# Three score blocks of a head pair, side by side instead of two projection steps apart

## The chip, the cores and the metric

The kernel runs on one core of one Trainium2 chip. The metric is the device time of one execution in microseconds (us), the median of three runs.

The core has a matrix engine (TensorE, PE in the profile; PEld is its weight load), a vector engine (VectorE, DVE), a scalar engine (ScalarE, ACT), a general engine (GpSimd, POOL) and a queue engine that issues transfers (SyncE, SP). Each engine works through its own list of instructions in order, and waits where an instruction needs what another engine has not yet finished.

## What is computed

The program is one layer of a hybrid decoder trunk over 1024 positions of width 1024. The part that matters here is the second of its two token mixers, a gated linear attention in chunks:

```python
def step(state, chunk):
    qc, kc, lfc, vc = chunk
    cum = jnp.cumsum(lfc, axis=2)
    o_inter = jnp.einsum('bhtk,bhkv->bhtv', qc * jnp.exp(cum), state)
    rel = cum[:, :, :, None, :] - cum[:, :, None, :, :]
    decay = jnp.where(causal[:, :, None], jnp.exp(jnp.minimum(rel, 0.0)), 0.0)
    scores = jnp.einsum('bhtsk,bhsk->bhts', qc[:, :, :, None, :] * decay, kc)
    o_intra = jnp.einsum('bhts,bhsv->bhtv', scores, vc)
    ...
    return state, o_inter + o_intra
```

Queries q, keys k, forget gates f and values v come from projections of the normalised input (`proj = h @ w_in`). Beside this mixer there are a gated recurrence (RG-LRU), an output projection, and then an MLP with squared ReLU (1024 to 4096 to 1024). All inputs are float32.

## The kernel before

The 1024 positions are worked in two halves of 512 (c = 0, 1), and the 8 heads in 4 pairs (p = 0 to 3). So the mixer goes through 8 head pairs, one after the other; the names of their tiles carry both numbers (`sc_10` is c = 1, p = 0), and the text counts them 0 to 7 in the order of time (4c + p).

Every float32 product of the projections is made of three matmuls of reduced operands (lines 144, 145, 146: high by high, high by low, low by high). While pair i goes through its attention (`hgrn`), TensorE also makes the projections of pair i + 1. These are cut into steps by a generator (`stage`): a step is six such matmuls of 128x512 (of 128x256 in the value projection). `hgrn` calls `go(n)` to run n steps of the next pair's projections, and then places its own small matmuls. The tables `GO`, `GO_FIRST` and `GO_SECOND_HALF` say how many steps go before each of them. While the mixer runs, all matmuls are pinned (`pin`, line 141): TensorE takes them in exactly the order of the program text. The other engines' orders are made by a scheduler from priorities.

The score matrix of 128 by 128 of one chunk is built in levels. For distances inside a pair of positions and for two coarser levels there are three score blocks, each made by `blocks` (line 570): 32 matmuls with 32 columns of weights and 48 columns moving. On the chip each of these is two passes, so a block is 64 matmul records.

- The first block (here pt1) reads `q` and `kk`, the second (pt2) `qa` and `kb`, the third (pt8) `qb` and `kc`. Each goes to a PSUM bank of its own (pt1 and pt2 of the two banks `sc`, pt8 of the two banks `hg`).
- VectorE then takes the blocks out of PSUM into `dd` with masks (`own_block`, lines 560 and 581; `level_blocks`, line 589), and at the same time it rewrites `kc`, `qb`, `kk` and `qf` for the next, coarser level. GpSimd copies `dd` into `scT` (line 675).
- After `at[1]` further steps come the blocks of the two coarsest levels (line 690, 32 columns wide; line 701, 64 columns wide), then the transposes of `kk` (`pk`, line 727), the products with v (`pkv`, line 737) and the outputs (`po`, lines 762 and 765).

In the first half the table has 26, so pt1 comes after 22 steps, pt2 after 24 and pt8 after 26. From pair 1 on, the first 16 of these steps are the value projection, the next 8 `xa`, and then `q` follows; `f` and the recurrence's gates (`pr`, `pi`) come behind. In the last pair, gates `g` and `mb` stand in the place of `xa` and what follows it.

Of the kernel before, what the change touches and what calls it, by code (L numbers as in the profile page):

```python
# [35 lines left out]
GO = (26, 5, 3, 1, 1)  # L36
GO_FIRST = (16, 5, 2, 1, 2)
GO_SECOND_HALF = (26, 7, 3, 1, 1)


PV_LB, PV_CB, PV_BR, PV_BI, PV_LAM, PV_CW, PV_HG = 0, 8, 16, 24, 32, 40, 72
# [4 lines left out]
def trunk(ctx: ExitStack, tc: tile.TileContext, x, wts, mlp, pv, gains, mask_f, mask_u, out):  # L46
# [15 lines left out]
    def bank(tag, name):  # L62
        return ps.tile([P, 512], F32, tag=tag, name=name, bufs={"pj": 4, "sc": 2, "hg": 2}[tag])
# [3 lines left out]
    for i in range(NC * NPAIR):  # L67
        at = (0, 1, 2, 3, 4, 6, 5)
# [487 lines left out]
    def hgrn(c, p, got, go):  # L556
# [6 lines left out]
        def blocks(k_, rhs, name, tag="sc"):  # L563

            pt = bank(tag, f"sc{name}_{nm}")[:, : 8 * 48].rearrange("p (n t) -> p n t", n=8)
            for n in range(8):
                for b in range(4):
                    k = 4 * n + b
                    pin(
                        PE.matmul(  # L570
                            pt[32 * b : 32 * b + 32, n, :], k_[:, 32 * k : 32 * k + 32], rhs(k), start=True, stop=True
                        )
                    )
            return pt
# [48 lines left out]
        def level_q(q4, t4, g, cw):  # L623
            mul(q4[:, :, 5, :], q4[:, :, 3, :], t4[:, :, 2:3].to_broadcast([P, g, cw]))
            mul(q4[:, :, 4:7:2, :], q4[:, :, 2:6:3, :], t4[:, :, 1:2].unsqueeze(3).to_broadcast([P, g, 2, cw]))
# [20 lines left out]
        q4 = qb.rearrange("p a (b c) -> p a b c", c=c1)  # L646
        level_q(q4, t4, g1, c1)
        at = GO_FIRST if first else GO_SECOND_HALF if c else GO
        between = 2
        go(at[0] - 2 * between)  # L650
        pt1 = blocks(kk, lambda k: q1[:, 16 * k : 16 * k + 16, :], "1")
        go(between)
        pt2 = blocks(kb, lambda k: qa[:, k * g0 // 32 : (k + 1) * g0 // 32, 1:7, :], str(c0))
        go(between)
        pt8 = blocks(kc, lambda k: q4[:, k * g1 // 32 : (k + 1) * g1 // 32, 1:7, :], str(c1), "hg")
        before, after = sums(t4, g1)
        mul(k4(kc, c1)[:, :, 0:3, :], k4(kc, c1)[:, :, 0:3, :], after.unsqueeze(3).to_broadcast([P, g1, 3, c1]))
# [23 lines left out]
                op1=ALU.add,  # L681
            )

        go(at[1])
        pt = bank("hg", f"sc32_{nm}")[:, :256].rearrange("p (n t) -> p n t", n=8)
        for n in range(8):
            for b in (0, 2):
# [70 lines left out]
        for s, u in both:  # L758
            for n in range(4):
# [3 lines left out]
                if not only:  # L763
                    at = s * T + n * P
# [177 lines left out]
    for i in range(NC * NPAIR):  # L942
        rest = stage(i + 1) if i + 1 < NC * NPAIR else last_stage()
        hgrn(*where(i), gots[i], lambda n: run(rest, n))
        run(rest)
# [704 lines left out]
```

## Time and profile before

| what | us |
|---|---|
| median of 3 runs | 1545.02 |
| lowest and highest of the 3 | 1544.61, 1545.6 |
| profiled execution, first to last instruction | 1544.2 |
| TensorE busy in it | 1527.6 (99%) |
| VectorE busy | 1150.0 (74%) |
| ScalarE busy | 810.2 (52%) |
| GpSimd busy | 149.8 (10%) |

The profiled execution has no time of its own beside its span; the span counts from its first to its last instruction and lies 0.8 us below the median of the runs. The mixer takes about the first 560 us, then follow the rest of the gates, the output projection and the MLP. In the timeline a row is one instruction, or a run of like ones (x64), with its start and how long it took. Matmuls are pipelined: a new one starts before the last has ended, so the distance between two starts tells more than the time of one.

### The profile page before, as it was taken

The page shows a single profiled execution, that of the slowest core. Times are in us where ns is not written, and L with a number is a line of the kernel's source. Part 1 is how long each engine was busy: PE and PEld are TensorE (multiplying, and loading weights), DVE is VectorE, ACT ScalarE, POOL GpSimd, SP SyncE. Part 2 cuts the span into 40 slices and gives each one's busy share as a digit, 9 for nine tenths or more (in the row PEclk, how much of TensorE's full clock was granted, in tenths as well). Part 3 has the DMA queues.
Part 4 walks back from the last instruction along what each step waited for, and adds up shares of the span by engine and source line. Part 5 has one row for each costly group of instructions (what it writes and reads, how often), then busy time and mean ns, then how long its engine had stood idle before and what let it go on. Part 6 is the DMA issues. An engine that isn't in the chain of part 4 may idle for free. (4 is left out here: it accounts for less than half of the span.)

```text
span 1544.2 us, 23190 instructions
## 1 busy us (share of the span) xinstructions
PE 1527.6 (99%) x9081; PEld 1275.3 (83%) x9081; DVE 1150.0 (74%) x1656; ACT 810.2 (52%) x1341; POOL 149.8 (10%) x188
## 2 busy tenths in 40 slices
PE   8999999999999999999999999999999999999998
PEld 7878888888888887888888888888888788888886
DVE  5798595485675928786866568888788898888877
ACT  5647757568567435453533347766666721111115
POOL 1021210233515600000000000000000000000000
PEclk9999999999999999999999999999999999999999
DMA  7555455465664274432328323666666675666642
GB/s 285 188 173 192 151 190 182 151 218 172 236 212 158 96 286 164 164 135 84 137 94 314 151 109 143 267 247 246 244 249 248 228 312 224 249 252 250 252 186 109
DMA packets 81679, 306.82 MB, mean 199 GB/s; under 512 B 8481, under 2 KB 20897, under 8 KB 68642
## 3 DMA queue, kind: packets, MB, share of 16 engines
q1 hardware_dynamic: 77536, 292.75, 51.8%
q10 hardware_dynamic: 4034, 12.59, 2.1%
q8 instruction: 71, 1.16, 0.3%
q14 instruction: 38, 0.31, 0.1%
HBM read 201.50 MB, written 103.81 MB: 198 GB/s over the span
## 5 line engine op out<-in xcount | busy, mean ns | idle before, releaser
L1559 DVE TENSOR_TENSOR acc<-acc,dX 128x512 f32<-128x512 f32 x128 | 85.0, 683 | 28.6 <-PE dX L146 26.9
L87 ACT CAST wA<-q 128x512 fp32r<-128x512 f32 x46 | 28.6, 622 | 147.5 <-PE dX L146 101.7
L88 DVE TENSOR_TENSOR wL<-raw,wH 128x1024 fp32r<-128x1024 f32 x48 | 58.8, 1225 | 46.0 <-ACT wH L87 45.7
L87 ACT CAST wH<-raw 128x1024 fp32r<-128x1024 f32 x48 | 50.4, 1050 | 39.4 <-DMA raw<-wts_in 16.1
L1559 DVE TENSOR_TENSOR acc<-acc,dY 128x512 f32<-128x512 f32 x64 | 43.4, 685 | 13.1 <-PE dY L146 12.9
L144 PE MATMUL po<-wH,y 128*128 128x512 f32 x128 | 49.8, 393 | 0.0
L145 PE MATMUL po<-wL,y 128*128 128x512 f32 x128 | 49.8, 389 | 0.0
L146 PE MATMUL po<-wH,y 128*128 128x512 f32 x128 | 49.7, 390 | 0.0
L1420 ACT ACTIVATE b<-b 128x512 f32<-128x512 f32 x48 | 30.2, 630 | 32.2 <-DVE b L1419 32.0
L88 DVE TENSOR_TENSOR wA<-q,wA 128x512 fp32r<-128x512 f32 x46 | 31.5, 686 | 16.6 <-ACT wA L87 16.4
L108 ACT CAST wH<-raw 128x1024 fp32r<-128x1024 f32 x36 | 37.7, 1048 | 9.8 <-issue 3.7
L465 DVE SCALAR_TENSOR_TENSOR xc<-xp,pvt,xc 128x512 f32<-128x512 f32 x48 | 40.1, 846 | 1.1 <-ACT xc L449 1.1
L171 POOL TENSOR_TENSOR rstd_h<-rstd_h,mhalf 128x1 f32<-128x1 f32 x8 | 4.6, 584 | 371.9 <-DVE rstd_h L166 371.9
L981 DVE TENSOR_TENSOR s<-q,q 128x512 f32<-128x512 f32 x46 | 31.6, 686 | 4.4 <-DMA q<-mlp_in 4.0
L378 POOL TENSOR_TENSOR stt<-r,stt 128x256 fp32r<-128x256 f32 x16 | 19.9, 1261 | 127.6 <-ACT stt L377 115.4
L989 DVE TENSOR_TENSOR s<-q 128x512 f32<-128x512 f32 x46 | 31.6, 686 | 0.4
L1421 ACT ACTIVATE b<-b 128x512 f32<-128x512 f32 x48 | 30.2, 631 | 1.2
L769 ACT ACTIVATE on<-po 128x128 f32<-128x128 f32 x64 | 16.9, 278 | 26.1 <-PE po L765 26.0
L1071 DVE TENSOR_TENSOR gb<-gY,ge 128x512 f32<-128x512 f32 x14 | 9.7, 690 | 25.1 <-PE gY L146 25.1
L146 PEld LDWEIGHTS po<-wH,y 128*128 128x128 f32 x128 | 24.0, 188 | 5.1
L145 PEld LDWEIGHTS po<-wL,y 128*128 128x128 f32 x128 | 24.1, 188 | 4.8
L144 PEld LDWEIGHTS po<-wH,y 128*128 128x128 f32 x128 | 24.0, 188 | 4.7
(2546 smaller groups left out, 5448.9 us busy)
## 6 DMA issues: line engine op xcount, KB each, us to landing
q<-mlp_in SPq DMA_DIRECT2D x92, 512.0 KB, 3.8
raw<-wts_in SPq DMA_DIRECT2D x80, 512.0 KB, 4.9
rest<-wL SPq DMA_DIRECT2D x36, 512.0 KB, 2.9
wL<-rest SPq DMA_DIRECT2D x36, 512.0 KB, 4.2
hd<-ri SPq DMA_DIRECT2D x16, 256.0 KB, 3.7
od<-onT ACTq DMA_DIRECT2D x8, 512.0 KB, 7.3
cdT<-stT SPq DMA_DIRECT2D x16, 256.0 KB, 3.4
o<-od SPq DMA_DIRECT2D x4, 1024.0 KB, 6.8
```

What stands on the lines that cost most here:

```text
L87: keep(A.copy(h, src))
L88: ins = V.tensor_tensor(out=lo, in0=src, in1=h.bitcast(F32), op=ALU.subtract)
L108: A.copy(h, raw)
L144: pin(PE.matmul(o, ah, bh, start=first, stop=False, **how))
L145: pin(PE.matmul(o, ah, bl, start=False, stop=False, **how))
L146: pin(PE.matmul(o, al, bh, start=False, stop=last, **how))
L465: ins = V.scalar_tensor_tensor(xc[:, s, :], xp[:, j : j + T], pvt[:, PV_CW + 8 * j + u : PV_CW + 8 * j + u + 1], xc[:, s, :], op0=ALU.mult ...
L981: ins = V.tensor_tensor(out=sa[:, 0, :], in0=a21, in1=a22, op=ALU.add)
L989: V.tensor_tensor(out=sb[:, 0, :], in0=a21, in1=a11, op=ALU.add)
L1420: A.activation(b[:, at, :], b[:, at, :], AF.Relu, scale=-1.0 if at == 2 else 1.0)
L1421: A.activation(b[:, at, :], b[:, at, :], AF.Square)
L1559: V.tensor_tensor(out=dst, in0=dst, in1=banks[bk, pr], op=op)
```

## The change

The same matmuls, vector operations and transfers remain. A new table moves the three score blocks among the projection steps:

```diff
+SCORES_AT = {0: (0, 2, 2), 2: (3, 0, 0), 7: (3, 0, 0)}
...
         at = GO_FIRST if first else GO_SECOND_HALF if c else GO
-        between = 2
-        go(at[0] - 2 * between)
+        before_1, before_2, before_8 = SCORES_AT.get(4 * c + p, (0, 0, 0))
+        go(at[0] - 4 + before_1)
         pt1 = blocks(kk, lambda k: q1[:, 16 * k : 16 * k + 16, :], "1")
-        go(between)
+        go(before_2)
         pt2 = blocks(kb, lambda k: qa[:, k * g0 // 32 : (k + 1) * g0 // 32, 1:7, :], str(c0))
-        go(between)
+        go(before_8)
         pt8 = blocks(kc, lambda k: q4[:, k * g1 // 32 : (k + 1) * g1 // 32, 1:7, :], str(c1), "hg")
...
-        go(at[1])
+        go(at[1] + 4 - before_1 - before_2 - before_8)
```

| pair | steps before pt1, pt2, pt8: before | after |
|---|---|---|
| 0 | 12, 14, 16 | 12, 14, 16 |
| 1, 3, 4, 5, 6 | 22, 24, 26 | 22, 22, 22 |
| 2, 7 | 22, 24, 26 | 25, 25, 25 |

The blocks behind them (line 690 and on) keep their step in every pair, since the last line gives back what the others took.

On TensorE, in pair 4 (`sc_10`), the three blocks stood so among the projections of `xa` and `q`, with 12 matmuls of 128x512 between one block and the next:

```order
L146 MATMUL pj_xa_1_3558<-hT11H,wL_3429 128x512
L570 MATMUL sc_10_3607<-q_3187,kk_3384 32x48 x32
L144 MATMUL pj_xa_0_3557<-hT11H,wH_3428 128x512
...
L146 MATMUL pj_xa_1_3558<-hT11H,wL_3429 128x512
L570 MATMUL sc_10_3659<-qa_3395,kb_3397 32x48 x32
L144 MATMUL pj_q_0_3715<-hT10H,wH_3561 128x512
...
L146 MATMUL pj_q_1_3716<-hT10H,wL_3562 128x512
L570 MATMUL sc_10_3735<-qb_3401,kc_3409 32x48 x32
L144 MATMUL pj_q_0_3715<-hT10H,wH_3561 128x512
```

Now they stand so (line numbers are one higher, because of the new line of the table):

```order
L147 MATMUL pj_xa_1_3558<-hT11H,wL_3429 128x512
L571 MATMUL sc_10_3607<-q_3187,kk_3384 32x48 x32
L571 MATMUL sc_10_3640<-qa_3395,kb_3397 32x48 x32
L571 MATMUL sc_10_3673<-qb_3401,kc_3409 32x48 x32
L145 MATMUL pj_xa_0_3557<-hT11H,wH_3428 128x512
```

All 24 projection matmuls that stood between the blocks have gone behind the third.

On VectorE, in the same pair, the operations that take the blocks out of PSUM (`dd`) stood mixed with the convolution of the next pair (`xc`, line 465), ahead of the rewriting of `kc` and `qb`:

```order
L581 COPY_PREDICATED dd_3392<-mu,sc_10_3607 128x128
L463 COPY xp_3656<-xcar 128x3
L589 COPY_PREDICATED dd_3392<-mu,sc_10_3659 128x32x6
L465 SCALAR_TENSOR_TENSOR xc_3652<-xp_3653,pvt,xc_3652 128x512
L589 COPY_PREDICATED dd_3392<-mu,sc_10_3659 128x32x4
L465 SCALAR_TENSOR_TENSOR xc_3652<-xp_3653,pvt,xc_3652 128x512
L589 COPY_PREDICATED dd_3392<-mu,sc_10_3659 128x32x2
L465 SCALAR_TENSOR_TENSOR xc_3652<-xp_3653,pvt,xc_3652 128x512
L465 SCALAR_TENSOR_TENSOR xc_3652<-xp_3656,pvt,xc_3652 128x512
L463 COPY xp_4357<-xcar 128x3
L465 SCALAR_TENSOR_TENSOR xc_3652<-xp_3656,pvt,xc_3652 128x512
L560 TENSOR_TENSOR kc_3409<-kc_3409,seg_3394 128x32x24
```

Now they stand so:

```order
L582 COPY_PREDICATED dd_3392<-mu,sc_10_3607 128x128
L590 COPY_PREDICATED dd_3392<-mu,sc_10_3640 128x32x6
L590 COPY_PREDICATED dd_3392<-mu,sc_10_3640 128x32x4
L590 COPY_PREDICATED dd_3392<-mu,sc_10_3640 128x32x2
L561 TENSOR_TENSOR kc_3409<-kc_3409,seg_3394 128x32x24
L561 TENSOR_TENSOR qb_3401<-qb_3401,seg_3394 128x32x8
L561 TENSOR_TENSOR qb_3401<-qb_3401,seg_3394 128x32x16
L561 TENSOR_TENSOR kk_3384<-kc_3409,seg_3394 128x16x32
L561 TENSOR_TENSOR qf_3717<-qb_3401,seg_3394 128x16x32
L590 COPY_PREDICATED dd_3392<-mu,sc_10_3673 128x8x24
L464 COPY xp_3748<-xcar 128x3
L590 COPY_PREDICATED dd_3392<-mu,sc_10_3673 128x8x16
```

The convolution has moved behind the work on the three blocks. Ahead of the first of these rows, that is up to the last operation that pt8 needs, VectorE's order in this pair is as it was.

## The prediction

> **What bounds the kernel now.** I read the page's first part, then the busy times by stretch, then TensorE's waits. In the stretches the columns are the stretch, its length, and the busy time and count of each engine (PE, PEld, DVE, ACT, POOL), then the granted clock and the transfers.
>
> ```profile
> PE 1527.6 (99%) x9081; PEld 1275.3 (83%) x9081; DVE 1150.0 (74%) x1656; ACT 810.2 (52%) x1341; POOL 149.8 (10%) x188
> ...
> 75.00:560.00 485.00, 482.60 (x4433) 414.85 (x4432) 339.41 (x586) 304.76 (x618) 139.41 (x161) 1.00 0.53 182
> 560.00:1300.00 740.00, 738.25 (x3271) 606.70 (x3270) 568.68 (x693) 399.82 (x565) 4.64 (x8) 1.00 0.53 196
> ...
> PE po L762 <- DVE sn L748: 1.0, 1, 1.0
> PE dZ L145 <- DVE wA1230L L88: 0.5, 1, 0.5
> PE sc L701 <- DVE qf L560: 0.5, 1, 0.5
> ```
>
> TensorE is busy for 482.6 of the 485 us in which the head pairs run, and for 738.25 of the 740 us behind them, at full clock. It waits for almost nothing: behind its start the largest wait is 1.0 us. So what TensorE is given in this stretch sets the end, and time that it is spared there should reach the end nearly whole, since the 740 us that follow are full too and nothing in their order has moved. A wait that it is given costs the same way. But a busy share does not say how fast it goes; that is read from starts. Pair 4, from its first score block to its third:
>
> ```profile
> 327.64 0.39 PE L145 MATMUL pj_xa<-hT11L,wH 128*128 128x512 f32 x1
> 327.86 0.39 PE L146 MATMUL pj_xa<-hT11H,wL 128*128 128x512 f32 x1
> 328.18 0.89 PE L570 MATMUL sc<-q,kk 128*32 128x48 f32 x64
> 329.00 0.50 PE L144 MATMUL pj_xa<-hT11H,wH 128*128 128x512 f32 x1
> 329.34 0.40 PE L145 MATMUL pj_xa<-hT11L,wH 128*128 128x512 f32 x1
> ...
> 330.03 0.39 PE L145 MATMUL pj_xa<-hT11L,wH 128*128 128x512 f32 x1
> ...
> 331.62 0.39 PE L146 MATMUL pj_xa<-hT11H,wL 128*128 128x512 f32 x1
> 331.94 0.89 PE L570 MATMUL sc<-qa,kb 128*32 128x48 f32 x64
> ...
> 335.70 0.89 PE L570 MATMUL sc<-qb,kc 128*32 128x48 f32 x64
> ...
> L570 PE MATMUL sc<-q,kk x512: 206/206/230, 84.6 to 513.5; 128*32 128x48 f32 x171
> ```
>
> Undisturbed projections start every 0.227 us (330.03 to 331.62 are seven starts: 1.59 / 7). From block to block it takes 3.76 us, and again 3.76, with 12 projections between: 12 x 0.227 = 2.72. A block that stands alone therefore costs 3.76 - 2.72 = **1.04 us**. Its 64 records themselves, first start to last start, take 0.89 less the last one's own 0.206, that is **0.68 us**. The other **0.36 us** is the way in and out: the first record comes 0.32 us behind the last projection instead of 0.227, the first projection comes late, and the second comes 0.34 us behind the first.
>
> **The change, part by part.** It removes no instruction and no transfer. In pairs 1 to 7 the three blocks now have one way in and one way out between them instead of three. Two are spared in each of seven pairs, 14 in all; pair 0 keeps its 12, 14, 16. By the rows above that is worth 14 x 0.36 = 5.0 us, if a border between two score blocks costs nothing beyond the records' pace.
>
> In pair 2 the first block already shares a border, with the eight transposes of the input rows:
>
> ```profile
> 197.09 0.39 PE L146 MATMUL pj_xa<-hT00H,wL 128*128 128x512 f32 x1
> 197.32 1.03 PE L178 MATMUL xT_x<-ident,xn 128*128 128x128 f32 x8
> ...
> 198.43 0.39 PE L145 MATMUL pj_xa<-hT00L,wH 128*128 128x512 f32 x1
> ...
> 203.44 0.39 PE L146 MATMUL pj_xa<-hT01H,wL 128*128 128x512 f32 x1
> 203.67 1.03 PE L178 MATMUL xT_x<-ident,xn 128*128 128x128 f32 x8
> 204.63 0.89 PE L570 MATMUL sc<-q,kk 128*32 128x48 f32 x64
> ...
> 205.79 0.39 PE L145 MATMUL pj_xa<-hT01L,wH 128*128 128x512 f32 x1
> ...
> L178 PE MATMUL xT_x<-ident,xn x64: 270/273/421, 7.5 to 204.4; 128*128 128x128 f32 x64
> ```
>
> Eight transposes alone cost 1.34 - 2 x 0.227 = 0.89 us. With the score block behind them the two cost 2.35 - 0.45 = 1.90. Apart, by the same measure, the block costs 329.34 - 327.86 - 0.45 = 1.03, so together 1.92. Moving the block away from the transposes loses only 0.02 us. This says something more: sharing a border with transposes saved nearly nothing, so the 0.36 us belongs to going over from weights 128 columns wide to weights 32 wide and back, not to going over from one kind of work to another.
>
> What a border between two score blocks costs the trace does not show; two rows bound it. The eight transposes go to two PSUM banks: 1.03 less one's own 0.273 over seven distances is 0.108 us each, and 8 x 0.108 = 0.87 of the 0.89, so a change of bank at one width costs 0 to 0.02. The other end is the border of the two coarse blocks:
>
> ```profile
> 220.00 0.70 PE L690 MATMUL sc<-qb,kc 128*32 128x32 f32 x32
> 220.63 1.15 PE L701 MATMUL sc<-qf,kk 128*64 128x64 f32 x16
> ...
> L690 PE MATMUL sc<-qb,kc x256: 189/196/217, 100.1 to 531.5; 128*32 128x32 f32 x128
> ```
>
> The first block's own starts spread over 0.70 - 0.196 = 0.50 us, so 0.13 us pass from its last start to the next block's first, where its own distance is 0.50 / 31 = 0.02: the border costs 0.11. There the width changes as well, from 32 to 64 columns. In the change the width stays, and only bank and operands change, as with the transposes; so I take 0.02 us, near that end. 14 x 0.02 = 0.3 us. At 0.11 it would be 1.5. Less than nothing is hardly possible: at most the slow first records of a block could go, a few hundredths each, 0.3 us in all.
>
> [...]
>
> Next, whether the blocks' operands are there. pt8 moves 4 steps forward (5.4 us) in five pairs. pt8 needs the last write of `qb`:
>
> ```profile
> 207.47 0.69 DVE L560 TENSOR_TENSOR qb<-qb,seg 128x512 f32<-128x512 f32 x1
> ...
> 326.99 0.69 DVE L560 TENSOR_TENSOR qb<-qb,seg 128x512 f32<-128x512 f32 x1
> ...
> 512.87 0.89 PE L570 MATMUL sc<-q,kk 128*32 128x48 f32 x64
> ...
> 515.70 1.16 DVE L560 TENSOR_TENSOR qb<-qb,seg 128x512 f32<-128x512 f32 x1
> ```
>
> In pair 4 pt8 would start two blocks behind 328.18, at 329.54, and `qb` is ready at 327.68: 1.9 us to spare. In pair 2 the blocks start three steps later than 204.63 (3 x 1.36 = 4.1), so pt8 at about 210.1 against 208.16: 1.9. Pair 7 has the least: counted in the same way from 512.87 pt8 starts at about 518.3, against 516.86: 1.4. VectorE's order ahead of these writes is unchanged, so I put no wait here. Without that cover each us of lateness would hold all the pinned projections behind pt8.
>
> What is late next? VectorE and ScalarE do the work on the blocks first and the next pair's convolution after it. The tight consumer is `pk`:
>
> ```profile
> 347.36 1.28 ACT L537 ACT_TABLE_LOAD   x1
> ...
> 351.38 0.68 DVE L560 TENSOR_TENSOR kk<-kk,seg 128x512 f32<-128x512 f32 x1
> ...
> 352.18 0.82 PE L727 MATMUL pk<-ident,kk 128*128 128x128 f32 x6
> ...
> 332.90 0.44 DVE L589 COPY_PREDICATED dd<-mu,sc 128x192 f32<-128x192 uint8 x1 [2.20 <-PE sc L570]
> ```
>
> `kk` is ready at 352.06, 0.1 us ahead of `pk`. But its chain hangs on ScalarE's table load, and that on the convolution; and VectorE stood idle for 2.2 us waiting for the second block, which now comes at once. So the chain moves forward, not back: nothing added. SP's and POOL's queues issue the same transfers, with small shifts; TensorE waits for none of them in this stretch.
>
> **Sum.** 5.0 - 0.02 - 0.3 = 4.7 us spared. The profiled execution would span 1544.2 - 4.7 = 1539.5; the median of the runs lies 0.8 above its span, so **1540.3 us**.
>
> **The rivals.**
>
> 1. *Each border costs like that of the coarse blocks*, 0.11 us: pt2 and pt8 have waits of their own, as the line-701 block has. Against it: that block also changes width. 5.0 - 1.5 = 3.5 spared, 1541.5 us.
> 2. *The borders are not spared at all*: the 0.36 us comes from refilling TensorE's queue behind any block's waits. Then the new order changes nothing, 1545.0 us. Against it: the transposes, which wait too, come 0.23 us behind a projection, at the normal pace.
> 3. *`pk` waits.* GpSimd's own work moves behind the copies of `dd`, and where it runs VectorE is slower: one and the same operation took 1.49 us in pair 4 and 0.95 in pair 2:
>
> ```profile
> 339.30 1.49 DVE L560 TENSOR_TENSOR kc<-kc,seg 128x768 f32<-128x768 f32 x1
> ...
> 339.93 1.46 POOL L363 TENSOR_TENSOR r<-hT01H,hT01L 128x256 f32<-128x256 f32 x1
> ...
> 215.38 0.95 DVE L560 TENSOR_TENSOR kc<-kc,seg 128x768 f32<-128x768 f32 x1
> ```
>
> If that falls on the two `q` products and on `kk` (about 0.5 us each, 1.5), `pk` waits 1.4 us in pairs 4, 5 and 6: 4.2 back, 0.5 spared, 1544.5 us. Against it: the chain starts earlier.
>
> 4. *pt8 waits for `qb`* (slower). TensorE is pinned, so each us beyond the 1.4 to 1.9 us to spare is lost, in seven pairs. It takes back the gain from 0.7 us beyond (4.7 / 7), and the kernel is slower by more than 0.2% from 1.1 us beyond. With `qb` 3.5 us later, for instance under GpSimd's work, 1.6 x 7 = 11.2 is lost, net 6.5: 1551.5 us. Against it: nothing has moved ahead of `qb` in VectorE's order.
>
> **How the numbers follow.** Forecast 0.72, rival 1 0.14, rival 2 0.05, rival 3 0.05, rival 4 0.04. 0.2% is 3.1 us, about what a measurement of this kernel can tell from no change: faster means below 1541.9, slower above 1548.1. The forecast is faster in nearly all of its cases (0.70 of 0.72), rival 1, close to the bound, in 0.09 of 0.14. Faster 0.79; same 0.17 (the rest of those two, rivals 2 and 3); slower 0.04. The forecast's own range goes by the border: from 5.3 spared, with 0.9 for the scatter of the runs (1544.61 to 1545.6), 1538.8, to about 3.6 spared, 1541.4. To leave out no more than 2 in 10 I reach over rival 1 with some more lost to waits: 1538.8 to 1543.0.
>
> **What would show it.** In the profile after: three line-571 groups of 64 in one run of 192 records, about 0.68 us from one block's first start to the next's; a span shorter by 0.68 us per pair from pair 1 on; no new row among TensorE's waits for `qb` or `kk`. The step on the border is wrong if the blocks' starts lie over 0.75 us apart; the step on the operands if a wait of TensorE for VectorE appears in front of line 571; the step on passing through if the gain at 560 us is larger than at the end.

## The result, and the profile after

The changed kernel takes 1554.54 us (median of 5 runs, 1551.81 to 1555.76), the kernel before 1544.61 beside it: a ratio of 1.006, interval 1.0049 to 1.0071. It is slower by 9.9 us where 4.7 were to be spared. The profiled execution is the lowest of the five: 1551.81, with a span of 1550.0 against 1544.2 before. The readings below therefore explain 5.8 us; the other executions have more of the same or something else, which their spans alone do not tell. Their mean granted clock, 0.995 to 0.997 against 0.998 here, suggests that more time at a lowered clock is part of it.

First the borders. Pair 5 in the timeline of the changed kernel (start, duration, what; x64 are 64 records):

```profile
392.99 0.39 PE L147 MATMUL pj_xa<-hT11H,wL 128*128 128x512 f32 x1
393.31 0.89 PE L571 MATMUL sc<-q,kk 128*32 128x48 f32 x64
394.01 0.87 PE L571 MATMUL sc<-qa,kb 128*32 128x48 f32 x64
394.69 0.87 PE L571 MATMUL sc<-qb,kc 128*32 128x48 f32 x64
395.49 0.50 PE L145 MATMUL pj_xa<-hT11H,wH 128*128 128x512 f32 x1
395.83 0.40 PE L146 MATMUL pj_xa<-hT11L,wH 128*128 128x512 f32 x1
```

The blocks start 0.70 and 0.68 us apart, which is their own pace. By the measure of the prediction the three cost 395.83 - 392.99 - 0.45 = 2.39 us together, against 3 x 1.03 alone: 0.70 us spared in this pair, where 0.68 was forecast. Over seven pairs that would be 4.9 us. Measured farther behind the blocks, as the lead or lag of the same matmul in the two traces, pairs 2, 5 and 7 each gain 0.64 to 0.67 us.

Then TensorE's waits in the whole span (line waited at, releaser, us in total, times, longest):

```profile
PE sc L571 <- issue: 3.4, 2, 2.4
PE pj_xa L146 <- issue: 3.2, 1, 3.2
...
PE pj_xa L145 <- issue: 1.6, 1, 1.6
...
PE pk L728 <- DVE kk L561: 0.9, 1, 0.9
```

None of these rows stood in the profile before. Three of them name no engine: "issue" is idle time for which the profile shows no wait. Together they are 3.4 + 3.2 + 1.6 = 8.2 us, in four places: pair 1 behind the third block (1.6), pair 4 inside it (1.0), and pairs 3 and 6. The last two in the timeline:

```profile
268.85 0.50 PE L145 MATMUL pj_xa<-hT11H,wH 128*128 128x512 f32 x1
272.60 0.40 PE L146 MATMUL pj_xa<-hT11L,wH 128*128 128x512 f32 x1 [3.25 <-issue]
...
455.58 0.53 PE L571 MATMUL sc<-qb,kc 128*32 128x48 f32 x32
458.50 0.66 PE L571 MATMUL sc<-qb,kc 128*32 128x48 f32 x32 [2.38 <-issue]
459.09 0.80 PE L145 MATMUL pj_xa<-hT11H,wH 128*128 128x512 f32 x1
459.68 0.63 PE L146 MATMUL pj_xa<-hT11L,wH 128*128 128x512 f32 x1
460.11 0.63 PE L147 MATMUL pj_xa<-hT11H,wL 128*128 128x512 f32 x1
```

In pair 6 TensorE stands in the middle of the third block: 32 records, nothing for 2.4 us, and then the other 32 of the same block, with the same operands. In pair 3 it stands between two matmuls of one projection. So what was missing was not a block's operand, as far as the rows go. Behind pair 6's stand the projections start 0.43 us apart instead of 0.227. The busy times by stretch tell why (stretch, length, busy time and count of PE, PEld, DVE, ACT and POOL, then the granted clock and the transfers). Four us of the kernel before, and then of the changed one with the stretch behind the head pairs:

```profile
459.00:463.00 4.00, 4.00 (x79) 3.36 (x72) 3.96 (x4) 0.08 (x1) 3.92 (x4) 1.00 0.71 259
```

```profile
459.00:463.00 4.00, 4.00 (x18) 3.12 (x12) 3.72 (x8) 1.34 (x3) 0.00 (x0) 0.60 0.08 29
560.00:1300.00 740.00, 738.55 (x3279) 607.78 (x3278) 566.40 (x690) 400.89 (x567) 4.64 (x8) 1.00 0.53 199
```

The 0.60 is the mean of those 4 us: the granted clock was 0.50 from 458.8 to 462.2, and full before and behind. One start 0.36 us late and six 0.20 late make 1.6 us.

The parts read so far, -4.9 (borders, by pair 5) + 8.2 (stands) + 1.6 (clock) + 0.9 (`pk`), add up to +5.8 us, the difference of the two spans, but that exactness is luck. Set the starts of the same matmuls in both traces side by side. At pair 0's first block the changed kernel is 0.8 us ahead (83.81 against 84.59). Pairs 2, 5 and 7 gain 0.64 to 0.67 us each; pairs 1, 3, 4 and 6, which stand, lose 1.7, 2.7, 0.6 and 3.4, their spared borders taken off; around `pk` in pair 7 another 1.05 us are lost. From pair 0's first block to the first matmul of `gY`, behind the head pairs, it takes 488.07 us instead of 480.60, 7.5 more, and is then 6.7 us behind (571.88 against 565.19). Of these, 5.8 are left at the end. The 740 us behind 560 are as full as before, 738.55 against 738.25: what was lost was lost in the head pairs.

### The profile page after: what moved, and what is told of

It reads as the page before. It is cut to its first block, busy times and chain, and to the rows that moved or that the text cites. A ratio compares the mean times of both kernels' runs of the same rounds, so it can differ in the third digit from the quotient of the medians.

```text
span 1550.0 us, 23193 instructions
## 1 busy us (share of the span) xinstructions
PE 1524.6 (98%) x9081; PEld 1276.5 (82%) x9081; DVE 1148.2 (74%) x1656; ACT 810.7 (52%) x1341; POOL 151.6 (10%) x188
## 3 DMA queue, kind: packets, MB, share of 16 engines
q8 instruction: 71, 1.16, 0.3%
## 5 line engine op out<-in xcount | busy, mean ns | idle before, releaser
L676 POOL TENSOR_SCALAR scT<-dd 32x256 f32<-32x256 f32 x32 | 19.7, 617 | 129.3 <-DVE dd L590 82.5
```

## What the stands have in common

The page's row on the transfers that bring TensorE's instructions is the same before and after (transfers, MB, share of 16 engines):

```profile
q8 instruction: 71, 1.16, 0.3%
```

71 transfers, 1.16 / 71 = 0.016 MB each, for 2 x 9081 = 18162 records of TensorE: 255.8 records to a transfer, so about 256 instructions come in one piece. Now count the records ahead of each stand. These stretches go from the start of the changed kernel to the middle of each of the four (matmuls, then weight loads, in brackets):

```profile
0.00:144.50 144.50, 136.84 (x1113) 115.08 (x1113) 112.30 (x207) 88.12 (x154) 23.91 (x34) 1.00 0.58 206
0.00:272.20 272.20, 261.08 (x2258) 223.58 (x2259) 206.69 (x372) 169.91 (x311) 42.58 (x60) 1.00 0.55 194
0.00:333.50 333.50, 321.23 (x2767) 275.99 (x2768) 239.76 (x435) 208.32 (x385) 50.06 (x72) 1.00 0.54 188
0.00:458.30 458.30, 443.25 (x3913) 382.39 (x3914) 319.03 (x574) 289.99 (x551) 98.16 (x130) 1.00 0.56 193
```

From stand to stand 2291, 1018 and 2292 records; with the few others of TensorE's list, which these columns leave out, they are 2304, 1024 and 2304, that is 9, 4 and 9 times 256 exactly. All four stands lie where one piece ends and the next begins.

The traces also hold the times of the transfers themselves, and these show the link. The instruction transfers ahead of the four stands begin at 142.27, 270.15, 331.48 and 456.20 us and take 1.17, 0.98, 0.95 and 0.88; TensorE goes on 1.45, 1.46, 1.45 and 1.42 us behind their ends. The runs below have 26 more stands without a named releaser: in every one TensorE goes on 1.2 to 1.6 us behind the end of an instruction transfer, and the count of TensorE's records ahead of it leaves the same remainder when divided by 256.

The counts gave the theory to test. **Theory A**: three adjacent blocks are 384 instructions (192 matmul records and 192 weight loads), and go through at 0.68 / 128 = 0.0053 us each; 256 take 1.36 us. A projection is two instructions in 0.227 us. Where blocks fill most of a piece, TensorE uses it up before the next has been brought. **Theory B**: a late operand or buffer that is not shown as a wait. **Theory C**: adjacency as such costs, in whichever pair.

## The experiments

**Pair 1 five steps earlier.**

```diff
-SCORES_AT = {0: (0, 2, 2), 2: (3, 0, 0), 7: (3, 0, 0)}
+SCORES_AT = {0: (0, 2, 2), 1: (-5, 0, 0), 2: (3, 0, 0), 7: (3, 0, 0)}
```

> The change with pair 1's three score blocks five projection steps earlier, nothing else moved. Theory A (TensorE's instructions come in pieces of 256, 16 KB a transfer; three adjacent blocks are 384 short instructions, and where they use up a piece in under about 4.5 us the next one is not there; what counts is where a piece ends within the three blocks): in pair 1 the piece's end moves from about record 134 of the 384 to about record 210, so the 1.8 us that TensorE stands idle behind pair 1's blocks go, and the idle times of pairs 3, 4 and 6 (3.7, 1.2, 2.6 us) stay where they are in the order. The head pairs end 2.4 us earlier than in the change, a span of about 1547.6. Theory B (the third block, or what follows it, waits for an operand or a buffer that the profile does not show as a wait): the blocks now have 6.8 us less time for their operands, so pair 1's idle time is at least as long, a span of 1550 or more.

One run, 1560.18 us, span 1558.4. TensorE's waits:

```profile
PE xT_x L179 <- DVE dd L590: 4.4, 1, 4.4
PE sc L571 <- issue: 4.2, 2, 2.5
PE pj_xa L147 <- issue: 3.2, 1, 3.2
...
PE sc L571 <- ACT v L428: 1.4, 1, 1.4
```

The stand of pair 1 is gone, and those of pairs 3, 4 and 6 stand one matmul later in the order than in the change, 3.6, 1.9 and 2.7 us from start to start. But the span misses Theory A's 1547.6: the blocks now lie ahead of the transposes of the input rows, which then wait 4.4 us for VectorE's `dd`, and the second block waits 1.4 us behind ScalarE's `v`. Both are ordinary waits with a named releaser. The span is on Theory B's side of 1550, for reasons that are not Theory B's; the run by itself decides little.

**Every piece 128 instructions further on.**

```diff
-        for _ in range(5):
+        for _ in range(69):
             keep(PE.transpose(idle[:, :P], ident, ident))
```

> The change with 64 more idle transposes at the start (128 instructions more on TensorE, some 7 us), no order changed. Theory A: every piece of 256 instructions now ends 128 instructions earlier in the program, so the idle times change their pairs: the piece's end within the three blocks moves to about record 6 in pairs 1 and 3, 81 in pair 2, 156 in pair 4, 50 in pair 5, 196 in pair 6 and 59 in pair 7. Pair 6 loses its 2.6 us, pair 4 keeps at most 0.5 us, pairs 1 and 3 stand, and pairs 2, 5 and 7, which stood nowhere in the change, now stand 2 to 4 us each, inside or right behind the blocks. Theory B: the same pairs stand as in the change (1, 3, 4, 6), for the same times, since all operands keep their times to each other.

One run, 1569.23 us, span 1567.1. TensorE's waits, and the records ahead of the first two stands:

```profile
PE sc L571 <- issue: 8.7, 4, 3.4
...
PE pj_xa L146 <- issue: 2.4, 1, 2.4
```

```profile
0.00:217.90 217.90, 209.56 (x1749) 178.97 (x1750) 164.57 (x292) 133.16 (x240) 37.71 (x51) 1.00 0.55 196
0.00:277.30 277.30, 267.82 (x2258) 229.72 (x2259) 203.22 (x365) 168.81 (x310) 42.34 (x60) 0.99 0.53 188
```

Again 1018 counted records apart, 1024 with the others. Nothing among the head pairs' operations had been touched, yet the stands went to other pairs. The table gives, for both kernels, the record of the 384 at which a piece ends (from the count of the records; the next piece ends 256 further on, and the stands lie 4 to 9 records ahead of that point) and the stand, as the distance of the two neighbouring starts:

| pair | the change: piece ends at | stands | 64 more transposes: piece ends at | stands |
|---|---|---|---|---|
| 1 | 134 | 1.8 us | 6 | none |
| 2 | 209 | none | 81 | 2.6 us |
| 3 | 134 | 3.7 us | 6 | 1.1 us |
| 4 | 28 | 1.2 us | 156 | 2.8 us |
| 5 | 178 | none | 50 | 3.6 us |
| 6 | 68 | 2.6 us | 196 | none |
| 7 | 187 | none | 59 | 2.1 us |

That rules out Theory B, which has the same pairs stand. Theory A's own figures failed in two pairs: pair 1 did not stand, and pair 4 stood 2.8 us instead of at most 0.5. In pair 1 the transfer of the next piece began 2.6 us ahead of the first block (143.34 against 145.96), in pair 3, which stood with its piece ending at the same record, only with the first block (275.01 against 275.03). So a piece can be asked for while the slow projections ahead are still running; what makes that early or late was not shown.

**Adjacent only where no piece ends badly.**

```diff
-SCORES_AT = {0: (0, 2, 2), 2: (3, 0, 0), 7: (3, 0, 0)}
+SCORES_AT = {0: (0, 2, 2), 1: (0, 2, 2), 2: (3, 0, 0), 3: (0, 2, 2), 4: (0, 2, 2), 6: (0, 2, 2), 7: (3, 0, 0)}
```

> The three blocks are adjacent only in pairs 2, 5 and 7; pairs 0, 1, 3, 4 and 6 have their blocks two steps apart as before. Theory A: no idle time of TensorE over 0.5 us with the releaser 'issue' anywhere; each of the three pairs is spared 0.6 to 0.7 us, and pair 7 gives up to 1.2 us back to the wait of pk for kk: together 0.8 to 2.0 us below the kernel before, span 1542.3 to 1543.5, ratio 0.9988 to 0.9995. Theory C (adjacency itself costs, in whichever pair): slower than before, by about three sevenths of the 9.9 us of the change, that is 4 us, ratio 1.0027.

1543.40 us (11 runs) against 1545.26 before: 0.999, interval 0.9981 to 0.9999; profiled span 1541.7. No row of TensorE's waits has "issue"; `pk` waits 0.8 us in pair 7, as in the change. By the medians this is Theory A's 0.8 to 2.0 us (1.9) and not Theory C's 4 us of loss. The one profile is a weaker witness: its span lies below the expected 1542.3 to 1543.5, but 1.5 of the 2.5 us to the profile before lie ahead of the first score block, where nothing was changed, and from that block to the first matmul of `gY` it gains only 0.6 (479.98 against 480.60).

**The fetch by itself.** The kernel is only this, with `small` the score matmuls of 32 columns by 48:

```python
projections(64)
small(512)
projections(96)
...                          # 16 loads of 512 KB start here
projections(32)
small(512)
projections(160)
for _ in range(3):
    small(96)
    projections(160)
```

> No trunk at all: x is copied to the output, and TensorE gets runs of projections and two bursts of 512 score-like matmuls (2048 instructions each, operands loaded long before), the first with no other transfers, the second while 8 MB of weights are loaded; behind them three bursts of 96 such matmuls (384 instructions) between projections. Theory A: in a burst 256 instructions run in 1.36 us and TensorE then stands until the next piece has landed, again and again: 4.5 us per 256 in the quiet burst, 36 us in all instead of 10.9, and longer in the burst beside the loads. Theory B: the bursts run through at 5.3 ns per instruction, about 11 us each, since nothing is waited for.

The timeline from the quiet burst, and behind the "..." from the start of the one beside the loads:

```profile
22.47 1.90 PE L85 MATMUL sc<-x,x 128*32 128x48 f32 x159
26.10 1.56 PE L85 MATMUL sc<-x,x 128*32 128x48 f32 x128 [1.73 <-issue]
29.83 1.56 PE L85 MATMUL sc<-x,x 128*32 128x48 f32 x128 [2.16 <-issue]
33.83 1.84 PE L85 MATMUL sc<-x,x 128*32 128x48 f32 x128 [2.44 <-issue]
...
88.90 2.24 PE L85 MATMUL sc<-x,x 128*32 128x48 f32 x128 [4.10 <-issue]
95.09 2.79 PE L85 MATMUL sc<-x,x 128*32 128x48 f32 x128 [3.96 <-issue]
```

With no operand to wait for, TensorE does 128 matmuls and their 128 weight loads and stands, again and again. The pieces follow each other in 3.73 and 4.00 us here, 3.45 to 4.00 in the whole quiet burst (4.5 was expected), and in 6.19 us beside the loads (5.7 for the piece before, 83.24 to 88.90; the loads end at about 95 us, and from there it is 3.7 to 4.0 again). Of the three bursts of 96, which are 384 instructions each like the three blocks, one stood, for 1.6 us, and two did not. So a piece costs 1.36 us of work and 3.45 us or more of bringing. The 71 transfers for 18162 records fit pieces of that size. How much longer than 1.36 us a piece's work must last for no stand to show, the next run tests.

**How many long instructions a piece needs.** The same without a trunk, with groups of 256 instructions, each `scores` small matmuls and then `steps` projections:

```python
mixed(6, 48, 32)             # times, scores, steps
mixed(6, 56, 16)
mixed(6, 60, 8)
...                          # 32 loads of 512 KB start here
mixed(4, 56, 16)
mixed(4, 60, 8)
```

> No trunk: x is copied to the output, and TensorE gets groups of 256 instructions, each group some score-like matmuls and then some projections, operands loaded long before: first, without other transfers, six groups of 48 and 32 (48 x 4 + 32 x 2 = 256 instructions), six of 56 and 16, six of 60 and 8; then, while 16 MB of weights are loaded, four of 56 and 16 and four of 60 and 8. By their own pace (5.3 ns per short instruction, 0.227 us per projection, 0.36 us for the way in and out) the groups take 8.6, 5.2 and 3.4 us. Theory A: a group takes its own time or the time of a fetch, whichever is longer. Quiet, where a fetch took 3.5 to 4.0 us: 8.6, 5.2 and 3.5 to 4.0 us, nothing stands in the first two kinds. Beside the loads, where fetches of up to 6.2 us were seen: 5.2 to 6.2 us and 4 to 6.2 us, standing in the last kind in each group. If fetches have no part in it: 8.6, 5.2, 3.4, and the same beside the loads.

Two neighbouring groups of each of the three quiet kinds, then the second kind beside the loads:

```profile
22.15 1.23 PE L89 MATMUL sc<-x,x 128*32 128x48 f32 x96
30.78 1.23 PE L89 MATMUL sc<-x,x 128*32 128x48 f32 x96
...
88.45 1.40 PE L89 MATMUL sc<-x,x 128*32 128x48 f32 x112
93.67 1.40 PE L89 MATMUL sc<-x,x 128*32 128x48 f32 x112
...
141.24 1.76 PE L89 MATMUL sc<-x,x 128*32 128x48 f32 x120
144.97 1.76 PE L89 MATMUL sc<-x,x 128*32 128x48 f32 x120
...
194.99 0.40 PE L89 MATMUL sc<-x,x 128*32 128x48 f32 x17 [0.32 <-issue]
...
201.19 0.40 PE L89 MATMUL sc<-x,x 128*32 128x48 f32 x17 [0.79 <-issue]
```

Quiet, a group takes 8.63, 5.22 and 3.73 us: the first two are their own pace, the third (3.45 by its own pace, as its first group had it) lies within the 3.45 to 4.00 us that a piece took in the quiet burst. Beside the loads, at 406 GB/s in the profile's slices, the second kind takes 6.20 us from 194.99 to 201.19 instead of 5.22, and stands in each group but the first. The third kind beside loads stays untested: the loads had ended by then, and it took 3.5 to 3.8 us as before.

**Half the instructions, the same borders.** In the change, and in the kernel before as its twin:

```diff
-            for n in range(8):
+            for n in range(0, 8, 2):
...
-                            pt[32 * b : 32 * b + 32, n, :], k_[:, 32 * k : 32 * k + 32], rhs(k), start=True, stop=True
+                            pt[32 * b : 32 * b + 32, n : n + 2, :], k_[:, 32 * k : 32 * k + 32], rhs(k), start=True, stop=True
...
```

Further down in the same diff the moving operand of each of the three calls of `blocks` becomes twice as wide.

> The change with every second score matmul left out and the others twice as wide (96 columns; half of the scores are not computed), so a head pair's three adjacent blocks are 192 instructions instead of 384. To be set against the same edit of the kernel before (blocks two steps apart). Theory A: no stretch of 256 instructions is short of projections any more, so TensorE stands nowhere with the releaser 'issue', and what the prediction promised for the borders shows: this kernel is 3.5 to 4.7 us faster than its twin (seven pairs at 0.66, less up to 1.2 for the wait of pk in pair 7). Theory C (adjacency itself costs): this kernel is slower than its twin, or at best level with it.

> The kernel before with every second score matmul left out and the others twice as wide (half of the scores are not computed): the twin of the run above. Both theories: no idle time with the releaser 'issue'; it is between 2 us slower and 15 us faster than the kernel before, depending on what a score matmul of 96 columns takes, which no row shows. It serves only as the other side of the comparison.

Adjacent 1539.30 us (9 runs, at most 1542.3), apart 1544.82 (10 runs, at least 1543.28); against the kernel before 0.9968 (0.9958 to 0.9977) and 1.0001 (0.9992 to 1.001). With 192 instructions instead of 384 the adjacent blocks are faster by 5.5 us, in the profiled spans by 3.0 (1542.1 to 1539.1), where 3.5 to 4.7 were expected. In the two profiles the stretch that was changed, from the first score block to the first matmul of `gY`, is 2.4 us shorter (478.03 against 480.41); the spread of the rest, which holds the same work, is as large, so the size of the gain is known less well than its direction. Neither has a wait with "issue"; `pk` waits 1.1 us in pair 7 of the adjacent one. The order that loses 9.9 us with 384 short instructions gains with 192: Theory C is out, and so is every wait that hangs on the blocks' place alone.

**A version that beats both.** Two blocks adjacent, the third where the kernel before has it, except in pairs 2 and 5:

```diff
-SCORES_AT = {0: (0, 2, 2), 2: (3, 0, 0), 7: (3, 0, 0)}
+SCORES_AT = {0: (0, 2, 2), 1: (0, 0, 4), 2: (3, 0, 0), 3: (0, 0, 4), 4: (0, 0, 4), 6: (0, 0, 4), 7: (0, 0, 4)}
```

> All scores. In pairs 1, 3, 4, 6 and 7 the first two blocks are adjacent where the change has them, and the third stands four steps later, where the kernel before has it; pairs 2 and 5 keep three adjacent blocks, pair 0 is as before. Theory A, with the rule that the runs so far give (the time between the moment when the last 64 instructions ahead of a piece begin and the piece's own end must be at least about 7.5 us beside weight loads): the shortest such time is 6.9 us in pairs 1, 3 and 6, so no idle time or at most 0.6 us in one of them; one border spared in five pairs (0.34 each) and two in two pairs (0.67 each), together 3.0 us below the kernel before, ratio 0.9975 to 0.9990, and faster than the version with pairs 2, 5 and 7 alone. Theory C: the more adjacent blocks the slower, above the kernel before.

1542.65 us (11 runs) against 1544.90: 0.9986, interval 0.9977 to 0.9995; profiled span 1539.9. Pair 6, which lost most in the change:

```profile
449.08 0.89 PE L571 MATMUL sc<-q,kk 128*32 128x48 f32 x64
449.79 0.88 PE L571 MATMUL sc<-qa,kb 128*32 128x48 f32 x64
...
456.26 0.89 PE L571 MATMUL sc<-qb,kc 128*32 128x48 f32 x64
```

No "issue" appears among TensorE's waits, and the 2.2 us are in the expected band, below the 3.0 of its account; a wait of `pk` of 0.6 us, now in pair 1, is part of the rest. From the first score block to the first matmul of `gY` the profile gains 1.7 us (478.90 against 480.60). Against the version with pairs 2, 5 and 7 alone it is 0.75 us lower by medians taken at different times, too little to tell the two apart.

## Why the prediction was wrong

**Right: the price of a border.** 0.36 us for each way in and out, about 0.02 for a border at one width: 0.64 to 0.70 us per undisturbed pair, by either measure, against 0.68. From block to block it takes 0.68 to 0.70 us (pairs 4, 5 and 6) where the 64 records themselves take 0.68, and rival 1 with its 0.11 us is out.

**Right: the operands.** No row shows a block waiting for `qb` or `kk`. One block did wait for something that the prediction left out: in pair 1 the third block starts 0.99 us behind the second (142.39 against 141.40), just when VectorE has read the transposes of the input rows out of a bank `hg` (`hT10L`, 141.65 to 142.34). That is 0.3 us, too short for the list of waits, and over the 0.75 us that the prediction had set as the sign of a costly border; a border it is not. Rival 4's 1551.5 us is not far from the result, and its mechanism is not there: a number near the truth is no support.

**Right: passing through.** Most of what the head pairs lost is still lost at the end, 5.8 us of the 6.7; the stretch behind them is as full as before. Rival 2, with nothing spared, is out.

**Wrong: "what TensorE is given in this stretch sets the end, and time that it is spared there should reach the end nearly whole".** This took for granted that a full TensorE always has its next instruction. The sum had terms for the pace of records, borders and operands, and none for how fast the instructions themselves arrive; no rival had one either. The change did not alter how many there are, but how closely 384 of them stand. The missing term measured 8.2 us of stands plus 1.6 of lowered clock in the profiled execution, against 4.7 to be spared. In the kernel before, 24 instructions of projections stood on either side of the middle block, 2.7 us each time, and that was the cover for the fetch: the 12 matmuls between blocks which the prediction took out as neutral.

**Wrong: "the chain moves forward, not back: nothing added" for `pk`.** It was worked out in pair 4 and taken for all. In pair 7 the blocks begin three steps later than before, and `pk` waits 0.85 us:

```profile
542.19 0.68 DVE L895 TENSOR_TENSOR g<-g,g 128x512 f32<-128x512 f32 x1
542.79 0.68 DVE L561 TENSOR_TENSOR kk<-kk,seg 128x512 f32<-128x512 f32 x1
```

VectorE has no gap there, and `kk` ends at 543.47, just as `pk` starts (543.53). It is rival 3's wait in a pair that rival 3 did not name (it had pairs 4 to 6) and from another cause. In the last version, where pair 7's first block keeps its old step and its third too, that wait did not appear; the three steps and the adjacency were not tried apart in this pair.

**What would have shown it in the profile before.** Three rows that were there: 71 instruction transfers for 18162 records, a block's 64 records in 0.68 us, and two projections' records in twice 0.227. Together they say that 256 instructions last 1.36 us in a block and 29 us in projections; the row's share gives about 1 us for a transfer itself (0.3% of 16 x 1544.2 us, over 71). How long a piece takes from its request until it can be used could not be read there, since nothing waited for it, and it should have stood among the rivals with that unknown as its price.

## What to carry to other kernels

Short instructions needed long ones among them: where a tightly packed run of small matmuls, longer than one instruction piece (256 here, matmuls and weight loads both counted), stood in these runs, it was limited by the bringing of instructions, 3.45 to 4.00 us a piece when quiet and 5.7 to 6.2 beside the loads, and not by the engine's 1.36. So before packing small matmuls together, count their instructions per piece and put the time of that piece beside those figures; and where idle time has no releaser, count records from one stand to the next before looking for a late operand. Spreading small work between large may look like a cost at its borders (0.36 us for a way in and out here) and still be what hides the fetch, as it did in the kernel before, where no wait had "issue".

## What was not expected of the hardware

- The place of a stand went by the count of instructions from the start: 64 transposes at the start moved the stands from pairs 1, 3, 4 and 6 to pairs 2, 3, 4, 5 and 7.
- The price varied with other traffic: 3.45 to 4.00 us from piece to piece when quiet, 5.7 to 6.2 beside the loads. The change's five runs spread over 4 us (1551.81 to 1555.76); that varying fetches make this spread was not shown.
- A stand of 2.4 us in pair 6 was followed by a granted clock of 0.50 for 3.4 us (458.79 to 462.20), which cost 1.6 us more; one of 3.25 us in pair 3 was followed by a clock of 1.00 and the full pace (272.60 and 272.83 are 0.23 us apart):

```profile
272.60 0.40 PE L146 MATMUL pj_xa<-hT11L,wH 128*128 128x512 f32 x1 [3.25 <-issue]
272.83 0.40 PE L147 MATMUL pj_xa<-hT11H,wL 128*128 128x512 f32 x1
```

Of these two stands the shorter was followed by the lower clock, the longer was not; what decided it was not shown.
